# Twelve gate and up slices of layer 0's second half as seven block products, with the weight blocks added in SBUF by VectorE

## The chip, the cores and the metric

The kernel runs on one core of one Trainium2 chip. The metric is the device time of one execution in microseconds (us). Inside the core TensorE (PE) multiplies matrices into the eight PSUM banks, VectorE (DVE) and ScalarE (ACT) do elementwise work, GpSimd (POOL) and SyncE (SP) mainly issue DMA transfers here. Each engine works off its own instruction stream in order and waits on semaphores for the others.

## The reference: what is computed

One inference step of a two-layer decoder, for a prompt of 1024 tokens and 8 sample tokens, all in float32, with a model width of 1024. Each layer has a mixer (layer 0: a gated linear recurrence beside attention over 256 memory tokens; layer 1: stick-breaking attention beside memory attention) and then a SwiGLU feed-forward block, with RMSNorm around both:

```python
def swiglu(h, w_gu, w_down):
    gate, up = jnp.split(h @ w_gu, 2, axis=-1)
    return (jax.nn.silu(gate) * up) @ w_down

h = h + rmsnorm(mix, g[1])
h = h + rmsnorm(swiglu(rmsnorm(h, g[2]), w_gu[l], w_down[l]), g[3])
```

The feed-forward width is 2816, so `w_gu` has 2 x 2816 columns and `w_down` has 2816 rows. The change concerns `h @ w_gu` of layer 0 for half of the tokens.

## The kernel before

Tokens are worked on in two groups: group 0 holds prompt tokens 0 to 511, group 1 holds prompt tokens 512 to 1023 and the 8 sample tokens (520 columns, worked as two pieces of 260). Activations lie with the model width on the 128 partitions, in eight tiles of 128 rows.

Every float32 operand is kept as two halves in a reduced-precision matmul type: a high half (a copy that rounds) and a low half (what is left). A product of two such operands is three matmuls: high x high, high x low, low x high. Activations are split once by `split_to`. Weights are split as they are loaded, by `split_w`: a DMA on SP's queue brings 128 x 512 numbers (256 KB) into a tile `w` of the pool `wraw` (5 buffers), ACT copies the high half into a tile `ws` of the pool `wspl` (5 buffers; L260), and DVE subtracts to give the low half (L261).

The feed-forward block is cut into 22 slices of 128 columns, in five parts of 5, 5, 4, 4 and 4 slices (`PARTS`). For each slice of a part a plain slice does: gate product (`proj`, L274, 48 matmuls of 260 columns), SiLU from exp and ln (`silu`, L291 to L295), up product (another 48), product of the two (L703), split of the result into a tile `m` (L281, L282). After the slices of a part comes the down projection of the part: eight output blocks m, each with three matmuls per slice and piece, added into `r` by DVE (L447).

At the end of the kernel, layer 1's group 1 does slices 4 to 21 in another form (`ffn_w`, `gate_up_w`). Gate and up weights of a slice are seen as a 2 x 2 matrix of blocks (two halves of the model width, 512 rows each, by gate and up), and the activations as a 2 x 2 matrix (two halves of the width by two pieces of 260 tokens). The product takes seven block products instead of eight (Winograd's form of Strassen's scheme). Each block product j (0 to 6) is 12 matmuls of 260 columns (L552). Sums of activation blocks are made once by `sums_w`. Sums of weight blocks have been put into DRAM far ahead, by accumulating DMAs on POOL's queue (`weight_sums`): they run beside layer 0's group 1 feed-forward block, one step per generator call, each started by a tiny ACT copy (`rr`, L602) and a tiny POOL copy (`mk`, L603). The four PSUM accumulators of a slice are single banks, and the bank order is arranged so that ACT and DVE move partial sums between them while other products run.

The order of instructions is not that of the source. Python generators are woven together (`weave`), and a scheduler then orders each engine's stream by priorities and by its own estimate of when operands will be ready. What it settles on is fixed when the program is built: an engine that waits for its next instruction does not take a later one.

The stretch that the change touches, in the profile of before: group 1 of layer 0 does parts 0 and 1 beside the attention of layer 1's group 0 (`b0.sb`, `b0.mem`); then parts 2, 3 and 4 (slices 10 to 21), with only `weight_sums` beside them. The memory attention `mem_attn` has, for each pair of query blocks, scores (L862), a row maximum on DVE (L867), exp on ACT (L873), a scale on DVE (L879), transposes on PE (L889) and values (L903). PSUM is split into two two-bank tiles `mm`, three single banks `s` and one bank `ns`.

Of the kernel before, what the change touches and what calls it, by code (L numbers as in the profile page):

```python
# [9 lines left out]
F32 = mybir.dt.float32  # L10
F32R = mybir.dt.float32r
# [7 lines left out]
P = 128  # L19
# [5 lines left out]
def tile_decoder(  # L25
# [61 lines left out]
    def Q(i):  # L87
        return single[0].tile([P, 512], F32, tag=f"q{i}", name=nm("q"))
# [6 lines left out]
    def A(dt=F32):  # L95
        return apool.tile([P, 2, WID], dt, tag="a", name=nm("a"))
# [226 lines left out]
            out.append(x)  # L323
            yield

    def sums_w(xs, ops):

        n, h = NG[1], PW[1]  # L330
        for k in range(4):
            x0, x1 = xs[k], xs[k + 4]
            y = YT()
            if k % 2 == 0:
                z, u = YT(), YT()
            o = (k % 2) * h

            def full(x, c):
                t = B()
                nc.vector.tensor_add(t[:, :h], x[:, 0, c : c + h].bitcast(F32), x[:, 1, c : c + h].bitcast(F32))  # L340
# [13 lines left out]
            yield  # L354

    def YT():
        return xpool.tile([P, 2, NG[1]], F32R, tag="x0", name=nm("y"))

    def wo_tiles(g):
# [91 lines left out]
    class out_proj:  # L451


        def __init__(self, g, l, store, last=False):
            self.g, self.l, self.store, self.x, self.last = g, l, store, [], last
# [65 lines left out]
        split_to((mt[:, 0, :n], mt[:, 1, :n]), sg[:, :n])  # L521
        return mt, last

    def gate_up_w(l, f, ops, spl, raws):

        h, n = PW[1], NG[1]
        part, o = part_of(f)
        gate, up = f * P, DFF + f * P
        src = [
            (w_gu[l][0:512, gate : gate + P], 0), (sums[l][part][0][:, o : o + P], 4), (sums[l][part][1][:, o : o + P], 5),  # L530
            (w_gu[l][512:D, gate : gate + P], 1), (sums[l][part][2][:, o : o + P], 6), (sums[l][part][3][:, o : o + P], 2),
            (w_gu[l][512:D, up : up + P], 3),
        ]

        def weight(j):
            r = raws()
            nc.sync.dma_start(r, src[j][0].rearrange("(k p) m -> p k m", p=P))
            return r.rearrange("p k m -> p (k m)")

        def split(src):  # L540
            w = spl()
            nc.scalar.copy(w[:, 0, :], src)  # L542
            nc.vector.tensor_sub(w[:, 1, :], src, w[:, 0, :].bitcast(F32))  # L543
            return w

        def product(ps, j, first=False):
            w = split(weight(j))
            i = src[j][1]
            for k in range(4):
                x = ops[k][i]  # L550
                for wi, (wj, xi) in enumerate(((0, 0), (0, 1), (1, 0))):
                    nc.tensor.matmul(  # L552
                        ps[:, :h], w[:, wj, k * P : (k + 1) * P], x[:, xi, :],
                        start=(first and k == 0 and wi == 0), stop=(k == 3 and wi == 2), skip_group_check=True,
                    )

        pa, pb, pc, pd = (Q(i) for i in range(4))
        product(pa, 0, True)
        nc.scalar.activation(pb[:, :h], pa[:, :h], AF.Copy, scale=-1.0)
        product(pd, 1, True)  # L560
        product(pb, 2)
        nc.scalar.activation(pc[:, :h], pb[:, :h], AF.Copy, scale=-1.0)
        product(pa, 3)
        sg = T()
        nc.scalar.activation(sg[:, :h], pa[:, :h], AF.Silu)
        product(pb, 4)
        dt = T()
        nc.scalar.copy(dt[:, h:n], pd[:, :h])
        gt = T()
        nc.vector.tensor_add(gt[:, h:n], dt[:, h:n], pb[:, :h])  # L570
        product(pc, 5)
        nc.vector.tensor_sub(gt[:, :h], pc[:, :h], dt[:, h:n])
        product(pb, 6)
        nc.scalar.activation(sg[:, h:n], gt[:, :h], AF.Silu)
        nc.vector.tensor_mul(sg[:, :h], sg[:, :h], pb[:, :h])
        nc.vector.tensor_mul(sg[:, h:n], sg[:, h:n], gt[:, h:n])
        mt = M(F32R)
        split_to((mt[:, 0, :n], mt[:, 1, :n]), sg[:, :n])
        return mt

    sums = {}

# [32 lines left out]
    class ffn_w:  # L615


        def __init__(self, l, x, plain):
            self.g, self.l, self.x, self.ops, self.plain, self.n, self.r, self.pi = 1, l, x, [], plain, 0, 0, 0
            self.R = self.acc = None  # L620
            self.half = []
            self.sums = sums_w(x, self.ops)

        def spl(self):
            self.n += 1
# [13 lines left out]
        def part(self, pi):  # L639
            l, n, h = self.l, NG[1], PW[1]  # L640
            f0, nf = PARTS[pi]
            last = pi == len(PARTS) - 1
            mids = []
            for j in range(nf):
                self.pi = pi
                if f0 + j < self.plain:
                    mt, ins = gate_up_q(l, f0 + j, self.x)
                    mids.append(mt)
                    with tc.issue_after(ins.ins):
                        for _ in range((1, 2, 1, 0)[j]):  # L650
                            next(self.sums, None)
                else:
                    mids.append(gate_up_w(l, f0 + j, self.ops, self.spl, self.raws))
                yield
            if pi == 0:
                self.R = R_one()
            if last:
                self.acc = small([P, WID], tag="st", bufs=3)
                nc.scalar.preload_act_table_set("natural_log_exp_and_others")
            for m in range(ND):  # L660
                w = split_w(w_down[l], f0, nf, m * P)
                pp = [Q(2 * (m % 2) + a) for a in range(2)]
                for k in range(nf):
                    wh, wl = w[k]
                    for wi, (wt, xi) in enumerate(((wh, 0), (wh, 1), (wl, 0))):
                        for a in range(2):
                            nc.tensor.matmul(  # L667
                                pp[a][:, :h], wt, mids[k][:, xi, a * h : (a + 1) * h],
                                start=(k == 0 and wi == 0), stop=(k == nf - 1 and wi == 2),
                            )  # L670
                for a in range(2):
                    d = self.R[m][:, a * h : (a + 1) * h]
                    if pi == 0:
                        nc.scalar.copy(d, pp[a][:, :h])
                    else:
                        nc.vector.tensor_add(d, d, pp[a][:, :h])
                if last:
# [8 lines left out]
            yield from finish_rows(self)  # L686

    class ffn:
        def __init__(self, g, l, xt, rows=False):
            self.g, self.l, self.xt, self.rows = g, l, xt, rows  # L690
            self.R = self.acc = None

        def part(self, pi):
            g, l = self.g, self.l
# [2 lines left out]
            last = pi == len(PARTS) - 1  # L697
            mids = []
            for j in range(nf):
                pg = proj(g, w_gu[l], 0, ND, (f0 + j) * P, self.xt)  # L700
                sg = silu(None, pg, g)
                pu = proj(g, w_gu[l], 0, ND, DFF + (f0 + j) * P, self.xt)
                nc.vector.tensor_mul(sv(sg, g), sv(sg, g), pv(pu, g))  # L703
                mt = M(F32R)
                split_to((mt[:, 0, :n], mt[:, 1, :n]), sg[:, :n])
                mids.append(mt)
                self.now = sg[:, 0:1]
                yield
            if pi == 0:
                self.R = R_one()  # L710
            if last:
                self.acc = small([P, WID], tag="st", bufs=3)
            for m in range(ND):
# [3 lines left out]
                if last and self.rows:  # L717
# [3 lines left out]
                    if m == 3:  # L721
                        first_half(self)
                if m % 2:
                    yield

        def finish(self, store):
# [770 lines left out]
    b0 = mixer_b(0, xb0)  # L1497
    weave((b0.heads(), 8), (o1.finish(), 17))
    b0.open()
    f1 = ffn(1, 0, o1.x)  # L1500
    ws = weight_sums(1, range(5), lambda: f1.now)
    weave((chain(b0.sb(), b0.mem()), 24), (chain(f1.part(0), f1.part(1)), 18), (islice(ws, 16), 17))
    weave((chain(f1.part(2), f1.part(3), f1.part(4)), 24), (ws, 24))
# [55 lines left out]
```

## Time and profile before

| | |
|---|---|
| median of 3 runs | 2498.44 us (2496.12 to 2499.25) |
| the profiled execution's own time | 2499.1 us |
| its span | 2497.4 us |
| PE busy | 2462.8 us (99%), 15565 matmuls |
| DVE busy | 1571.8 us (63%) |
| ACT busy | 1183.0 us (47%) |
| DMA | 358.21 MB, 143 GB/s mean |

The span is from the first to the last instruction of one profiled execution; its own time has 1.7 us around that. Busy time is a union of the instructions' durations. A matmul's duration is its latency; since matmuls overlap, the pace is read from start to start. Views used below: busy time by stretches of time, groups of instructions by line, the chain of work that ended last, instructions in order of time, and DMA issues with their time to landing.

### The profile page before, as it was taken

What the parts mean: (1) busy time and instruction counts of PE and PEld (TensorE: products, weight loads), DVE (VectorE), ACT (ScalarE), POOL (GpSimd) and SP (SyncE); (2) the same over time, 40 slices, a digit from 0 to 9 for tenths busy, and PEclk for the clock granted to TensorE, in tenths of its full rate; (3) what the DMA queues carried; (4) which work ended last, traced back from release to release, by engine and by line L of the source; (5) the groups of instructions that cost most, each with busy time, mean ns of one, the idle gap of its engine ahead of it and who ended that gap; (6) DMA issues with size and microseconds to landing.
All of it is one profiled execution on the core that took longest, in us unless ns stands there. A gap on an engine that the chain in (4) does not pass through costs nothing.

```text
span 2497.4 us, 40764 instructions
## 1 busy us (share of the span) xinstructions
PE 2462.8 (99%) x15565; PEld 2169.9 (87%) x15565; DVE 1571.8 (63%) x2756; ACT 1183.0 (47%) x2277; POOL 98.3 (4%) x139
## 2 busy tenths in 40 slices
PE   8999999999999999999999999999999999999998
PEld 6888988877877897999999989877787797999997
DVE  5766556655765585655544575777577648755655
ACT  5446543243433454555433454555444445564444
POOL 1000000000000000010111100022000000000000
PEclk9999999999999999999999999999999999999999
DMA  5352252233643447586678976544454234365542
GB/s 186 114 165 68 72 156 81 60 110 116 184 124 98 129 138 227 156 195 177 173 191 215 234 193 196 160 142 138 121 149 130 85 115 122 121 192 145 151 137 69
DMA packets 496110, 358.21 MB, mean 143 GB/s; under 512 B 19110, under 2 KB 443635, under 8 KB 495915
## 3 DMA queue, kind: packets, MB, share of 16 engines
q1 hardware_dynamic: 477354, 301.08, 40.5%
q0 software_dynamic: 18560, 54.53, 9.1%
q8 instruction: 122, 2.00, 0.3%
q14 instruction: 74, 0.60, 0.1%
HBM read 325.73 MB, written 75.94 MB: 161 GB/s over the span
## 4 chain that ended last, share of the span: by engine, by line
PE 88%; DVE 5%; DMA 3%; ACT 2%; issue 2%; POOL 0%; SPq 0%; DVEq 0%; ACTq 0%; POOLq 0%
PE mm L274 59%; PE q L552 7%; PE q L667 5%; PE s L1180 2%; PE q L510 2%; PE mm L1048 2%; PE s L903 1%; PE s L862 1%; PE mm L812 1%; DMA b<-qd 1%; PE mm L839 1%; DVE ws L261 1%; PE ns L957 1%; PE s L1336 1%; DMA c<-in_cache_sb_v,pidx 1%
## 5 line engine op out<-in xcount | busy, mean ns | idle before, releaser
L274 PE MATMUL mm<-x,ws 128*128 128x260 f32 (+1 forms) x7776 | 1332.9, 330 | 0.0
L274 PEld LDWEIGHTS mm<-x,ws 128*128 128x128 f32 x7776 | 1148.3, 188 | 151.5 <-issue 12.0
L260 ACT CAST ws<-w 128x512 fp32r<-128x512 f32 x712 | 420.2, 591 | 763.2 <-PE mm L274 620.2
L261 DVE TENSOR_TENSOR ws<-w,ws 128x512 fp32r<-128x512 f32 x712 | 462.5, 653 | 286.8 <-ACT ws L260 278.3
L274 PE MATMUL mm<-m,ws 128*128 128x512 f32 (+1 forms) x2112 | 393.5, 343 | 0.1
L274 PEld LDWEIGHTS mm<-m,ws 128*128 128x128 f32 x2112 | 324.4, 189 | 49.9 <-issue 2.6
L667 PE MATMUL q<-m,ws 128*128 128x260 f32 x1056 | 128.8, 283 | 0.0
L667 PEld LDWEIGHTS q<-m,ws 128*128 128x128 f32 x1056 | 127.2, 188 | 0.4 <-ACT hT L485 0.2
L543 DVE TENSOR_TENSOR ws<-w,ws 128x512 fp32r<-128x512 f32 x126 | 86.6, 691 | 61.5 <-ACT ws L542 59.3
L552 PE MATMUL q<-y,ws 128*128 128x260 f32 x864 | 112.9, 283 | 0.0
L542 ACT CAST ws<-w 128x512 fp32r<-128x512 f32 x126 | 78.0, 621 | 69.6 <-PE q L667 27.4
L552 PEld LDWEIGHTS q<-y,ws 128*128 128x128 f32 x864 | 107.6, 189 | 0.0
L291 DVE TENSOR_SCALAR t<-mm 128x512 f32<-128x512 f32 (+1 forms) x82 | 56.7, 692 | 79.6 <-PE mm L274 79.6
L447 DVE TENSOR_TENSOR r<-r,mm 128x512 f32<-128x512 f32 (+1 forms) x96 | 66.0, 688 | 61.1 <-PE mm L274 60.3
L703 DVE TENSOR_TENSOR t<-t,mm 128x512 f32<-128x512 f32 (+1 forms) x66 | 45.5, 690 | 74.2 <-PE mm L274 73.9
L295 DVE TENSOR_TENSOR t<-t,t 128x512 f32<-128x512 f32 (+1 forms) x66 | 45.8, 694 | 70.6 <-ACT t L294 70.6
L552 PE MATMUL q<-x,ws 128*128 128x260 f32 x648 | 86.3, 282 | 0.0
L552 PEld LDWEIGHTS q<-x,ws 128*128 128x128 f32 x648 | 81.3, 188 | 0.0
L314 DVE TENSOR_TENSOR st<-st,n 128x512 f32<-128x512 f32 (+1 forms) x98 | 67.1, 691 | 8.8 <-ACT n L313 7.0
L281 ACT CAST m<-t 128x512 fp32r<-128x512 f32 (+1 forms) x88 | 54.9, 624 | 18.1 <-DVE t L703 8.9
L282 DVE TENSOR_TENSOR m<-t,m 128x512 fp32r<-128x512 f32 (+1 forms) x88 | 61.0, 693 | 2.6 <-ACT m L281 1.4
L984 POOL DMA_INDIRECT c<-in_cache_sb_k,pidx x16 | 16.4, 1026 | 1170.5 <-ACT n L313 958.6
(339 smaller groups left out, 2557.9 us busy)
## 6 DMA issues: line engine op xcount, KB each, us to landing
w<-in_w_gu SPq DMA_DIRECT2D x334, 256.0 KB, 3.4
w<-in_w_down SPq DMA_DIRECT2D x160, 256.0 KB, 3.5
w<-in_w_in_a SPq DMA_DIRECT2D x80, 256.0 KB, 3.0
wsum<-in_w_gu POOLq DMA_DIRECT2D x18, 1024.0 KB, 9.5
w<-wsum SPq DMA_DIRECT2D x72, 256.0 KB, 3.8
w<-in_w_o SPq DMA_DIRECT2D x64, 256.0 KB, 2.8
wsum<-in_w_gu POOLq DMA_DIRECT2D x12, 1280.0 KB, 10.7
w<-in_w_mem_kv SPq DMA_DIRECT2D x32, 256.0 KB, 3.2
```

What stands on the lines that cost most here:

```text
L260: nc.scalar.copy(ws[:, 0, :n, :], raw[:, :n, :])
L261: nc.vector.tensor_sub(ws[:, 1, :n, :], raw[:, :n, :], ws[:, 0, :n, :].bitcast(F32))
L274: nc.tensor.matmul(ps[:, a, : PW[g]], wt, xt[k][:, xi, o : o + PW[g]], start=(k == 0 and wi == 0), stop=(k == nk - 1 and wi == 2),)
L281: nc.scalar.copy(dst[0], src)
L282: nc.vector.tensor_sub(dst[1], src, dst[0].bitcast(F32))
L291: nc.vector.tensor_scalar(sv(x, g), pv(ps, g), -44.0, None, op0=ALU.max)
L314: nc.vector.tensor_add(acc[:, :n], acc[:, :n], t[:, :n])
L447: nc.vector.tensor_add(dst, dst, pv(ps, g))
L542: nc.scalar.copy(w[:, 0, :], src)
L543: nc.vector.tensor_sub(w[:, 1, :], src, w[:, 0, :].bitcast(F32))
L552: nc.tensor.matmul(ps[:, :h], w[:, wj, k * P : (k + 1) * P], x[:, xi, :], start=(first and k == 0 and wi == 0), stop=(k == 3 and wi == 2), ...
L667: nc.tensor.matmul(pp[a][:, :h], wt, mids[k][:, xi, a * h : (a + 1) * h], start=(k == 0 and wi == 0), stop=(k == nf - 1 and wi == 2),)
```

## The change

The class `ffn` of layer 0 gets a number `prod`, the first slice to be done as block products; group 1 of layer 0 is made with `prod=10`, so parts 2, 3 and 4 use them. `gate_up_w` is made general: it is given a function that yields the weight block for product j, and a function that yields the four accumulators. For layer 0 these are:

- `sums_here`: the four weight blocks a11, a12 (gate), a21, a22 (up) of a slice are loaded in four DMAs of 256 KB into two tiles `c` of the pool `cpool` (4 buffers, shared with attention), one with a11 and a12, one with a21 and a22. DVE makes the sums: a21+a22, a11+a21, the latter plus a22, and that plus a12, in four tiles `b` of the pool `bpool`.
- accumulators: two single banks `s` and the two halves of a two-bank tile `mm`.
- `sums_w` is run for the activations of layer 0's group 1 too, during the down projection of part 1, into tiles `a` of the pool `apool`.
- The SiLU of these slices is ACT's own function, as in layer 1, so ACT's function table is loaded once before and once after.

Everything after layer 0 is unchanged but for the names of arguments. The loads of the paged cache for layer 1 (`cache_sb_k`, POOL's queue), which use `cpool` too, come out later in POOL's stream: before, eight of them stood ahead of and among the sums of weights; now these eight stand among the last sums.

```diff
-    def gate_up_w(l, f, ops, spl, raws):
...
+    def sums_here(l, f, raws, outs):
+        a11, a12, a21, a22 = raws()
+        for r, k0, m0 in (
+            (a11, 0, f * P), (a21, 0, DFF + f * P), (a12, 512, f * P), (a22, 512, DFF + f * P),
+        ):
+            nc.sync.dma_start(
+                r.rearrange("p (k m) -> p k m", m=P), w_gu[l][k0 : k0 + 512, m0 : m0 + P].rearrange("(k p) m -> p k m", p=P)
+            )
+        kept = {}
+
+        def add(a, b):
+            t = outs()
+            nc.vector.tensor_add(t, a, b)
+            return t
+
+        def weight(j):
+            if j == 1:
+                return add(a21, a22)
+            if j == 2:
+                kept[3] = add(a11, a21)
+                kept[2] = add(kept[3], a22)
+                return kept[2]
+            if j == 4:
+                return kept[3]
+            if j == 5:
+                return add(kept[2], a12)
+            return (a11, None, None, a12, None, None, a22)[j]
+
+        return weight
+
+    def gate_up_w(weight, ops, spl, quads):
...
-        pa, pb, pc, pd = (Q(i) for i in range(4))
+        pa, pb, pc, pd = quads()
...
     class ffn:
-        def __init__(self, g, l, xt, rows=False):
-            self.g, self.l, self.xt, self.rows = g, l, xt, rows
+        def __init__(self, g, l, xt, rows=False, prod=NF):
+            self.g, self.l, self.xt, self.rows, self.prod = g, l, xt, rows, prod
             self.R = self.acc = None
+            self.ops = []
+            self.sums = sums_w(xt, self.ops, lambda: A(F32R))
+
+        def raws(self):
+            ts = [C(), C()]
+            return [t[:, a, :] for t in ts for a in range(2)]
+
+        def quads(self):
+            t = mmp.tile([P, 2, 512], F32, tag="mm", name=nm("mm"))
+            return S(), t[:, 0, :], t[:, 1, :], S()
...
+                if f0 + j >= self.prod:
+                    mt, gate = gate_up_w(
+                        sums_here(l, f0 + j, self.raws, B),
+                        self.ops, lambda: wspl.tile([P, 2, 512], F32R, tag="ws", name=nm("ws")), self.quads,
+                    )
+                    mids.append(mt)
+                    self.now = mt[:, 0, 0:1].bitcast(F32)
+                    yield
+                    continue
...
+            if last and self.prod < NF:
+                with tc.issue_after(gate.ins):
+                    nc.scalar.preload_act_table_set("natural_log_exp_and_others")
...
                 if m % 2:
+                    if f0 + nf == self.prod < NF:
+                        next(self.sums, None)
                     yield
...
-    f1 = ffn(1, 0, o1.x)
+    f1 = ffn(1, 0, o1.x, prod=10)
```

More of the change, by code (lines that the diff above doesn't have):

```diff
@@ L324, in normed, with sums_w @@
             yield
-    def sums_w(xs, ops):
+    def sums_w(xs, ops, YT):
         n, h = NG[1], PW[1]
@@ L354, in sums_w, with Y0 @@
             yield
-    def YT():
+    def Y0():
         return xpool.tile([P, 2, NG[1]], F32R, tag="x0", name=nm("y"))
@@ L522, in gate_up_q, with sums_stored @@
         return mt, last
-    def gate_up_w(l, f, ops, spl, raws):
-        h, n = PW[1], NG[1]
+    def sums_stored(l, f, raws):
         part, o = part_of(f)
         gate, up = f * P, DFF + f * P
+        s1, s2, s3, s4 = (t[:, o : o + P] for t in sums[l][part])
         src = [
-            (w_gu[l][0:512, gate : gate + P], 0), (sums[l][part][0][:, o : o + P], 4), (sums[l][part][1][:, o : o + P], 5),
-            (w_gu[l][512:D, gate : gate + P], 1), (sums[l][part][2][:, o : o + P], 6), (sums[l][part][3][:, o : o + P], 2),
-            (w_gu[l][512:D, up : up + P], 3),
+            w_gu[l][0:512, gate : gate + P], s1, s2, w_gu[l][512:D, gate : gate + P], s3, s4,
+            w_gu[l][512:D, up : up + P],
         ]
@@ L536, in weight @@
             r = raws()
-            nc.sync.dma_start(r, src[j][0].rearrange("(k p) m -> p k m", p=P))
+            nc.sync.dma_start(r, src[j].rearrange("(k p) m -> p k m", p=P))
             return r.rearrange("p k m -> p (k m)")
+        return weight
[24 more added lines that the diff above has]
+            return (a11, None, None, a12, None, None, a22)[j]
+        return weight
+    def gate_up_w(weight, ops, spl, quads):
+        h, n = PW[1], NG[1]
+        src = (0, 4, 5, 1, 6, 2, 3)
         def split(src):
@@ L547, in product @@
             w = split(weight(j))
-            i = src[j][1]
+            i = src[j]
             for k in range(4):
@@ L573, in gate_up_w @@
         product(pb, 6)
-        nc.scalar.activation(sg[:, h:n], gt[:, :h], AF.Silu)
+        last = nc.scalar.activation(sg[:, h:n], gt[:, :h], AF.Silu)
         nc.vector.tensor_mul(sg[:, :h], sg[:, :h], pb[:, :h])
@@ L578, in gate_up_w @@
         split_to((mt[:, 0, :n], mt[:, 1, :n]), sg[:, :n])
-        return mt
+        return mt, last
     sums = {}
@@ L621, in __init__ @@
             self.half = []
-            self.sums = sums_w(x, self.ops)
+            self.sums = sums_w(x, self.ops, Y0)
         def spl(self):
@@ L652, in part @@
                 else:
-                    mids.append(gate_up_w(l, f0 + j, self.ops, self.spl, self.raws))
+                    mids.append(gate_up_w(
+                        sums_stored(l, f0 + j, self.raws), self.ops, self.spl, lambda: [Q(i) for i in range(4)]
+                    )[0])
                 yield
```

## The prediction

> **What bounds the kernel now.** I read the page's totals first, then the chain that ended last over the stretch that the change touches, then busy time by stretches.
>
> ```profile
> span 2497.4 us, 40764 instructions
> PE 2462.8 (99%) x15565; PEld 2169.9 (87%) x15565; DVE 1571.8 (63%) x2756; ACT 1183.0 (47%) x2277; POOL 98.3 (4%) x139
> ```
>
> ```profile
> 1241.31 209.76 PE mm L274 x1730
> ```
>
> ```profile
> 1196.00:1241.00 45.00, 44.93 (x336) 42.60 (x334) 24.47 (x52) 19.17 (x51) 5.50 (x8) 1.00 0.76 182
> 1241.00:1450.00 209.00, 209.00 (x1729) 208.11 (x1728) 104.84 (x153) 84.49 (x154) 31.05 (x47) 1.00 0.84 213
> 2480.00:2497.00 17.00, 6.43 (x42) 4.69 (x40) 8.69 (x14) 5.20 (x9) 0.00 (x0) 0.65 0.32 125
> ```
>
> The columns of the last view are stretch, length, busy time and count of PE, PEld, DVE, ACT and POOL, granted clock, DMA share, GB/s. From 1241 to 1451 us (parts 2 to 4 of layer 0's group 1, slices 10 to 21) the chain is 1730 matmuls and nothing else: TensorE never waits, and VectorE is half busy. Matmuls taken out here shorten the kernel one for one, as long as nothing new makes TensorE wait. The question is what does.
>
> **The change, part by part.**
>
> *Matmuls removed.* A slice drops from 96 matmuls to 84. Both forms stand in this trace: two plain slices by their L703, two product slices by their first products.
>
> ```profile
> 1250.19 0.70 DVE L703 TENSOR_TENSOR t<-t,mm 128x520 f32<-128x520 f32 x1 [1.51 <-PE mm L274]
> 1261.67 0.70 DVE L703 TENSOR_TENSOR t<-t,mm 128x520 f32<-128x520 f32 x1 [1.52 <-PE mm L274]
> ```
>
> ```profile
> 2299.79 3.06 PE L552 MATMUL q<-y,ws 128*128 128x260 f32 x24
> 2304.12 1.61 PE L552 MATMUL q<-y,ws 128*128 128x260 f32 x12
> 2305.57 1.60 PE L552 MATMUL q<-x,ws 128*128 128x260 f32 x12
> ...
> 2309.88 3.06 PE L552 MATMUL q<-y,ws 128*128 128x260 f32 x24
> ```
>
> 11.48 us against 10.09 us: 1.39 us a slice, for twelve slices **-16.7 us**. A product takes 1.45 us, a matmul 10.09 / 84 = 0.120 us.
>
> *Work added on VectorE and ScalarE.* Spacing of operations that follow each other at once:
>
> ```profile
> 1234.30 0.69 DVE L447 TENSOR_TENSOR r<-r,mm 128x520 f32<-128x520 f32 x1
> 1234.91 0.69 DVE L261 TENSOR_TENSOR ws<-w,ws 128x512 fp32r<-128x512 f32 x1
> 1235.51 0.68 DVE L282 TENSOR_TENSOR x<-s,x 128x512 fp32r<-128x512 f32 x1
> 1236.11 0.68 DVE L867 TENSOR_REDUCE nmx<-s 128x2 f32<-128x512 f32 x1
> ```
>
> ```profile
> 2308.46 0.42 DVE L576 TENSOR_TENSOR t<-t,t 128x260 f32<-128x260 f32 x1
> 2308.80 0.42 DVE L575 TENSOR_TENSOR t<-t,q 128x260 f32<-128x260 f32 x1
> ```
>
> ```profile
> L260 ACT CAST ws<-w 128x512 fp32r<-128x512 f32 x648 | 401.2, 620 | 665.2 <-PE mm L274 550.0 <-issue 34.0 <-PE mm L1048 12.3
> L517 ACT ACT_TABLE_LOAD x1 | 1.3, 1283 | 0.0
> ```
>
> So 0.6 us for 512 columns, 0.34 us for 260. A product slice has 12 of the first (seven splits, four adds, the split of `m`) and four of the second: 8.6 us of VectorE in 10.09 us. By throughput it fits, with 1.5 us to spare. ScalarE has eight casts and five short copies, about 7 us, and two table loads of 1.3 us; these hide behind the waits below, and would cost up to 2.6 us without them.
>
> *The weight loads.* This is the part that decides. `cpool` holds two slices. The tile with a21 and a22 of slice n is free only after VectorE's last split of that slice (a22, product 6); only then can SP load slice n+2 into it. On VectorE, in the built program, the add a21+a22 of slice n+2 stands five instructions behind that split, and ahead of everything that slice n+1 still needs:
>
> ```
> split a22 of slice 14          <- frees the tile, load of slice 16 starts
> splits 0, 1, 2 of slice 15, one 260-column add
> a21+a22 of slice 16            <- waits for that load
> a11+a21 of 16, a 260-column subtraction, +a22 of 16, split 3 of slice 15,
> a 260-column product, split 4, a 260-column product, split 5, +a12 of 16,
> split of m (slice 14), split a22 of slice 15
> ```
>
> The queue is in order, so each slice costs VectorE at least W, the wait from the one split to the landed pair of loads, plus what runs from that add to the next such split: nine operations of 0.6 us and three of 0.34 us, 6.5 us. W has no row of its own; the rows nearest are single loads of the same 256 KB in the same stretch, beside the sums of weights, and in the last stretch, without them.
>
> ```profile
> w<-in_w_gu SPq DMA_DIRECT2D x35, 256.0 KB, 6.7
> wsum<-in_w_gu POOLq DMA_DIRECT2D x16, 1024.0 KB, 9.3
> ```
>
> ```profile
> w<-in_w_gu SPq DMA_DIRECT2D x28, 256.0 KB, 3.4
> ```
>
> ```profile
> DMA to landing us min/median/max: 3.4/5.8/8.2
> ```
>
> ```profile
> GB/s 130 284 124 181 241 88 155 247 127 186 337 227 158 245 222 237 163 310 253 263 164 119 170 246 107 207 377 168 208 239 273 113 211 368 203 284 136 83 205 354
> ```
>
> Before, these loads run five buffers (some 14 us) ahead, and 6.7 us hurts nobody. Now W stands in a loop. I take 6.7 us for the first load and 0.7 us for the second behind it (256 KB at the 377 GB/s of the busiest slice): **W = 7.4 us**, because each tile is freed just as the slice's `m` starts the next sum of weights. Bounds: 4.1 us (3.4 + 0.7, no sum beside it) and 8.9 us (8.2 + 0.7). A turn is then 7.4 + 6.5 = 13.9 us, against the 10.09 us that TensorE needs and the 11.48 us of before.
>
> Worked through part 3 (slices 14 to 17), from its first product. Slices 14 and 15 were loaded during the down projection. Five `ws` buffers let split 6 of slice 14 follow the end of the second product: 2.9 + cast 0.62 + split 0.6 = 4.2 us. Then split 6 of slices 15, 16, 17 at 18.1, 32.0 and 45.9 us. The next add waits W again, for slice 19, and ahead of slice 17's last subtraction and products: four operations of 0.6 us, three of 0.34 us and a cast, 4.1 us, until slice 17's `m` is there at 45.9 + 7.4 + 4.1 = 57.4 us. TensorE, unhindered, asks for it after four slices and 24 matmuls of the down projection, 360 x 0.120 = 43.2 us. Loss: 14.2 us, about six of them in one piece at that end.
>
> Part 2 has one wait more: slice 11's tile is held by the memory attention until 2.3 us after its last scaling. From there 2.3 + W + 2.4 + W + 3.7 + W + 6.5 + W + 6.5 + W + 4.1 = 62.5 us (short runs first, since the queue is still filling), against 44.4 us: 18.1 us. Part 4 has nothing to load behind slice 21, so two waits: 4.2 + W + 6.5 + W + 4.1, and 1.8 us on ScalarE until product 4 of slice 20 has its accumulator, 31.4 us, against 216 x 0.120 = 25.9 us: 5.5 us. Sum: 18.1 + 14.2 + 5.5 = **+37.8 us**, which is 11 W - 43.6.
>
> *Sums of activations, end of the memory attention.* 48 operations of 260 columns, 16 us of VectorE, enter the stretch from 1196 to 1241 us, where 24.5 of 45 us are busy. They fit, but the attention's short chain queues behind them, and the plain matmuls that filled its gaps are gone:
>
> ```profile
> 1234.81 1.03 PE L862 MATMUL s<-c,a 128*128 128x256 f32 x4
> 1236.48 2.14 PE L274 MATMUL mm<-x,ws 128*128 128x260 f32 x15
> 1238.69 0.33 PE L889 MATMUL s<-ident,b 128*128 128x128 f32 x1
> ```
>
> Last scores (done at 1235.84) to transposes are 2.85 us; now only 0.5 us of values can stand in them: 2.3 us. The pair before gets about 1.2 us later by the operations put ahead of its maximum. **+3.5 us**; bounds 0 (all in VectorE's slack) and 16 (all on the path); I stay near the low end, since the slack of 20 us is larger than the work.
>
> *Moved.* SP issues as many loads as before; the last three of each down projection now stand behind the tile freed by the part's last split (45.9 us above), and are needed after 57 us: nothing. The cache loads on POOL move to about 1430 us and wait there for `c` tiles, with `mk` copies and sums of weights behind them; the next such load of before runs at 1615 us, and the sums are read after 2200 us: nothing.
>
> ```profile
> 1615.46 1.26 POOL L984 DMA_INDIRECT c<-in_cache_sb_k,pidx  x1 [157.49 <-DVE sc L944]
> ```
>
> Sum: -16.7 + 37.8 + 3.5 = +24.6 us on the profiled execution's 2499.1 us, which is 0.7 us above the median of the runs: **2524 us**.
>
> **The rivals.**
>
> *The loads land in time (faster).* If W stays under 5.2 us (11 x 5.2 - 43.6 - 16.7 + 3.5 = 0), the sign turns. For it: 3.4 us, the fastest load here and the median of the last stretch; slices get longer, so sums of weights lie less densely. Against: each load starts together with a sum, whose own 9.3 us cover it. At W = 4.1 us only part 2 loses, 1.5 us: 2499.1 - 16.7 + 1.5 + 3.5 = 2487 us.
>
> *In between.* W near 5.2 us: 2499 us.
>
> *Pairs queue.* Two pairs per slice are in flight together, and the sum is in the way of all of them. At W = 8.9 us: 2524 + 11 x 1.5 = 2540 us.
>
> *The clock falls in the waits.* In the last row of stretches above, with TensorE mostly idle, the granted clock is 0.65. If the two waits of some 6 us at part ends and the one of 4 us in slice 10 bring it there for as long again, matmuls in those 16 us take 1 / 0.65: +8.6 us, 2533 us. Against: no row of this trace shows it for waits that short. The Trainium skill (TensorE: Matmul & The Clock Gate, section "HAM oscillation — how this bites in real kernels") says that idle gaps above some 3.4 us, here those three, bring half clock; by its 3.4 us at half rate after each, an estimate, the sum would be 3 x 1.7 = 5 us more. No run shown yet can tell.
>
> *The change does not save its matmuls:* excluded by the 10.09 us that the same form takes in layer 1.
>
> **How the numbers follow.** Forecast 0.48 (W 6 to 8.2, 2509 to 2533 us); pairs queue 0.20; the clock 0.09; in between 0.08; in time 0.15, most of it clearly faster. A measurement of this kernel tells about 0.2% (5 us) from no change. Faster 0.14, same 0.08, slower 0.78. Range 2497 to 2541 us: from the middle case to the upper bound of W; it leaves out most of the faster case and the far ends.
>
> **What would show it.** Right: matmuls down by 144; the adds of a21+a22 wait for DMA, 2 to 5 us each, with TensorE's idle time in those parts ended by VectorE; product slices about 13.9 us apart; idle pieces of some 6 us before the down projections of parts 2 and 3; a span of the parts near 1241 to 1470 us. Wrong: products 1.45 us apart throughout, or those loads landing under 5 us; a lower granted clock between 1241 and 1480 us would speak for the fourth rival.

## The result, and the profile after

The changed kernel takes 2527.4 us (median of six runs, 2521.3 to 2532.4), the kernel before 2498.4 us (2496.1 to 2499.3): 1.0117 times as long, interval 1.0102 to 1.0133, so 29 us slower. The prediction was 2524 us. The profiled execution took 2524.87 us, its span is 2523.0 us, 25.6 us more than before. Totals of the page, then the stretches, with the columns of before:

```profile
span 2523.0 us, 40632 instructions
PE 2459.1 (97%) x15421; PEld 2162.1 (86%) x15421; DVE 1628.9 (65%) x2900; ACT 1206.7 (48%) x2355; POOL 98.3 (4%) x139
```

```profile
1196.00:1241.00 45.00, 43.49 (x321) 40.84 (x320) 38.32 (x95) 24.48 (x65) 2.18 (x4) 1.00 0.66 157
1241.00:1480.00 239.00, 209.18 (x1584) 202.96 (x1584) 145.28 (x247) 102.03 (x217) 37.73 (x54) 0.94 0.75 193
```

144 matmuls are gone, yet TensorE is busy only 3.7 us less: between 1241 and 1480 us it stands idle for 29.8 us, where in the kernel before it never stood until the parts were done, and its granted clock there is 0.94. The waits of that stretch (who waited for what: total, times, longest), and a piece of the chain that ended last in part 3:

```profile
DVE b L552 <- DMA c<-in_w_gu: 31.0, 10, 6.4
PE mm L587 <- DVE t L607: 28.3, 9, 6.3
```

```profile
1324.37 0.70 DVE ws L578
1325.50 4.63 DMA c<-in_w_gu
1330.22 1.29 DVE b L552 x2
...
1336.22 0.61 DVE ws L578
1337.26 6.32 DMA c<-in_w_gu
1343.68 1.29 DVE b L552 x2
...
1350.93 0.61 DVE ws L578
1351.97 6.27 DMA c<-in_w_gu
1358.33 1.29 DVE b L552 x2
...
1364.32 0.61 DVE ws L578
1365.36 9.43 DMA c<-in_w_gu
1374.89 1.29 DVE b L552 x2
```

This is the loop: last split of a slice (L578), load, add (L552), work to the next such split. From add to add it turns in 13.5, 14.7 and 16.6 us. From the end of the split to the add, the W of the prediction, are 5.2, 6.9, 6.8 and 10.0 us, 7.2 on average. TensorE's own rows, with the idle time before each in brackets:

```profile
1262.56 2.43 PE L587 MATMUL mm<-a,ws 128*128 128x260 f32 x12 [2.33 <-DVE t L607]
1276.85 2.95 PE L587 MATMUL mm<-a,ws 128*128 128x260 f32 x12 [2.21 <-DVE t L607]
1295.18 2.97 PE L587 MATMUL mm<-a,ws 128*128 128x260 f32 x12 [6.25 <-DVE t L607]
...
1345.36 2.97 PE L587 MATMUL mm<-a,ws 128*128 128x260 f32 x12 [2.91 <-DVE t L607]
1360.01 1.72 PE L587 MATMUL mm<-a,ws 128*128 128x260 f32 x12 [2.69 <-DVE t L607]
1376.58 2.97 PE L587 MATMUL mm<-a,ws 128*128 128x260 f32 x12 [6.01 <-DVE t L607]
...
1428.67 1.70 PE L587 MATMUL mm<-a,ws 128*128 128x260 f32 x12 [3.45 <-DVE t L607]
```

Every long wait stands before product 6, two of 6 us at the ends of parts 2 and 3. And in five of these seven rows the twelve matmuls behind the wait take 2.4 to 3.0 us, not the 1.7 us of the other two: these waits cost time twice, once as idle time and once in the matmuls behind them. What differs is the granted clock (third number from the end) in the stretches behind the waits, here two that cost twice and the one of 3.45 us that does not:

```profile
1295.10:1298.00 2.90, 2.82 (x13) 2.82 (x14) 1.56 (x4) 0.42 (x1) 0.00 (x0) 0.50 0.04 12
1376.50:1379.40 2.90, 2.83 (x13) 2.83 (x14) 1.56 (x4) 0.42 (x1) 0.00 (x0) 0.50 0.07 16
1428.60:1431.40 2.80, 2.73 (x22) 2.73 (x23) 2.80 (x7) 1.82 (x4) 1.29 (x1) 1.00 0.00 0
```

The stretch ends with the first matmul of the final norm (L303), which starts when part 4 is done; it is called the parts' end below. Before, then changed:

```profile
1450.90 1.02 PE L303 MATMUL ns<-st,ones 128*128 128x512 f32 x2
```

```profile
1478.97 1.02 PE L303 MATMUL ns<-st,ones 128*128 128x512 f32 x2
```

The parts end 28.1 us later; the rest of the kernel is 2.5 us shorter, and why stays open.

### The profile page after: what moved, and what is told of

Read it like the earlier page. It is cut to its first block, busy times and chain, and to the rows that moved or that the text cites. A ratio compares the mean times of both kernels' runs of the same rounds, so it can differ in the third digit from the quotient of the medians.

```text
span 2523.0 us, 40632 instructions
## 1 busy us (share of the span) xinstructions
PE 2459.1 (97%) x15421; PEld 2162.1 (86%) x15421; DVE 1628.9 (65%) x2900; ACT 1206.7 (48%) x2355; POOL 98.3 (4%) x139
## 4 chain that ended last, share of the span: by engine, by line
PE 86%; DVE 6%; DMA 4%; ACT 2%; issue 1%; SPq 0%; POOL 0%; DVEq 0%; ACTq 0%
PE mm L274 55%; PE q L587 7%; PE q L704 5%; DMA c<-in_w_gu 3%; PE s L1241 2%; PE q L510 2%; PE mm L1109 2%; PE s L964 1%; PE s L923 1%; DMA b<-qd 1%; PE mm L587 1%; PE mm L873 1%; PE ns L1018 1%; PE mm L900 1%; PE s L1397 1%
## 5 line engine op out<-in xcount | busy, mean ns | idle before, releaser
L274 PE MATMUL mm<-x,ws 128*128 128x512 f32 (+1 forms) x6624 | 1193.5, 338 | 0.0
L274 PEld LDWEIGHTS mm<-x,ws 128*128 128x128 f32 x6624 | 1009.4, 188 | 152.0 <-issue 12.0
L260 ACT CAST ws<-w 128x512 fp32r<-128x512 f32 (+1 forms) x664 | 390.3, 589 | 659.5 <-PE mm L274 511.1
L261 DVE TENSOR_TENSOR ws<-w,ws 128x512 fp32r<-128x512 f32 (+1 forms) x664 | 429.0, 649 | 269.6 <-ACT ws L260 264.8
L578 DVE TENSOR_TENSOR ws<-w,ws 128x512 fp32r<-128x512 f32 x126 | 86.5, 691 | 61.9 <-ACT ws L577 57.6
L577 ACT CAST ws<-w 128x512 fp32r<-128x512 f32 x126 | 77.9, 621 | 71.1 <-PE q L704 26.0
L587 PE MATMUL mm<-a,ws 128*128 128x260 f32 x432 | 64.8, 304 | 28.3 <-DVE t L607 28.3
L291 DVE TENSOR_SCALAR t<-mm 128x512 f32<-128x512 f32 (+1 forms) x70 | 48.3, 690 | 61.9 <-PE mm L274 61.7
L587 PEld LDWEIGHTS mm<-a,ws 128*128 128x128 f32 x432 | 59.6, 206 | 30.6 <-DVE t L607 30.1
L759 DVE TENSOR_TENSOR t<-t,mm 128x512 f32<-128x512 f32 (+1 forms) x54 | 37.2, 688 | 55.5 <-PE mm L274 55.0
L638 POOL COPY mk<-rr 128x1 f32<-128x1 f32 x40 | 14.7, 368 | 1343.8 <-ACT rr L637 1331.1
```

The source lines that it names most:

```text
L260: nc.scalar.copy(ws[:, 0, :n, :], raw[:, :n, :])
L261: nc.vector.tensor_sub(ws[:, 1, :n, :], raw[:, :n, :], ws[:, 0, :n, :].bitcast(F32))
L274: nc.tensor.matmul(ps[:, a, : PW[g]], wt, xt[k][:, xi, o : o + PW[g]], start=(k == 0 and wi == 0), stop=(k == nk - 1 and wi == 2),)
L587: nc.tensor.matmul(ps[:, :h], w[:, wj, k * P : (k + 1) * P], x[:, xi, :], start=(first and k == 0 and wi == 0), stop=(k == 3 and wi == 2), ...
```

## The experiments

All times are medians, the parts' ends are those of one profiled execution each; the kernel before took 2498.3 us beside e1 to e7, 2496.4 beside e8 and e9, 2498.5 beside e10 and e11.

| kernel | time, us | parts' end, us |
|---|---|---|
| before | 2498.4 | 1450.9 |
| changed | 2527.4 | 1479.0 |
| e1 add later | 2487.8 | 1441.8 |
| e2 deeper loads | 2494.9 | 1447.5 |
| e3 sums of weights later | 2510.6 | 1443.4 |
| e4 part 4 only | 2495.9 | 1449.9 |
| e5 sums of activations alone | 2497.8 | 1450.5 |
| e6 matmuls in the waits | 2533.2 | 1487.1 |
| e7 three delays (one run) | 2516.3 | 1472.0 |
| e8 three delays, filled | 2511.9 | 1468.0 |
| e9 add later, deeper loads | 2487.6 | 1439.6 |
| e10 other banks | 2519.7 | 1473.0 |
| e11 add later, other banks | 2491.1 | 1444.6 |

**e1: the place of the add.** In `sums_here`, with `last_split` set by `split`:

```diff
             if j == 1:
-                return add(a21, a22)
+                with tc.issue_after(last_split[0].ins) if last_split else ExitStack():
+                    return add(a21, a22)
```

> Everything is computed; only VectorE's order changes: the add a21+a22 of a slice is queued behind the last split of the slice before, so the wait for a landing no longer stands ahead of work that the slice before still needs. The loads, their buffers and the sums of weights stay as they are. Queue theory (the loss is the place of the add in an in-order queue): the load has some 10 us from one slice's last split to the next slice's, against landings of 5 to 10 us in the changed kernel, so the waits of DVE on c<-in_w_gu fall from 6.4 us to under 2 us, TensorE's 29.8 us of idle time between 1241 and 1480 us to under 6 us, and the time to 2498.4 - 16.7 (matmuls) + 3.5 (sums of activations) + 1.5 (slice 11's held tile) = 2487 us, range 2482 to 2496. Rival, the loads themselves are the limit (landings get as late as the queue allows): slices stay 13 us or more apart, 2515 to 2527 us. Rival, VectorE's 8.6 us of work in 10.09 us does not fit in practice: slices 10.6 to 11 us apart, 2493 to 2498 us, with idle time of TensorE ended by VectorE and no DMA behind it.

Measured: 2487.8 us, 0.9960 of before (0.9947 to 0.9972), faster than both kernels. In VectorE's waits no DMA is left, and TensorE is busy throughout (the three largest of VectorE's waits from 1241 to 1442 us; then the stretch):

```profile
DVE ws L261 <- ACT ws L260: 16.7, 17, 3.2
DVE r L447 <- PE mm L274: 14.5, 14, 1.5
DVE ws L581 <- ACT ws L580: 11.5, 21, 1.0
```

```profile
1241.00:1442.00 201.00, 199.98 (x1605) 195.87 (x1604) 148.38 (x251) 103.73 (x221) 37.40 (x53) 1.00 0.88 230
```

Loads, buffers, sums of weights and VectorE's operations are those of the changed kernel. Their order differs: with the add that the edit names, the other three adds of the slice stand behind the last split of the slice before, too. This place in the queue is worth 37.2 us at the parts' end. VectorE's 8.6 us of work in a turn of 10 us does fit: 148.4 of 201 us busy.

**e2: loads earlier, the add in its place.**

```diff
-            ts = [C(), C()]
-            return [t[:, a, :] for t in ts for a in range(2)]
+            t = C()
+            ws = [wraw.tile([P, 4, P], F32, tag="w", name=nm("w")) for _ in range(2)]
+            return [t[:, 0, :], t[:, 1, :]] + [w.rearrange("p k m -> p (k m)") for w in ws]
```

> Everything is computed; only the buffers of the raw weights change: a11 and a12 of a slice still share one tile of cpool, a21 and a22 take two of the five wraw buffers, so cpool holds four slices and wraw two and a half, and a21+a22 of slice n+2 no longer waits for the last split of slice n. Queue theory: the loop of split, load and add is cut at the load's start, so the same gain as with the add put later: 2487 us, range 2482 to 2496, no wait of DVE on c or w above 2 us. If the late add gives that gain and this one does not, loads started earlier do not help (they queue among themselves), and the place of the add is what counts. Rival, the loads are the limit: 2515 to 2527 us. One new wait is possible: loads of w_down now share wraw with a21 and a22; if they come late, idle time before the down projections ended by ws<-w, up to 3 us in each of three parts.

Measured: 2494.9 us, 0.9991 (0.9982 to 1.0001). 31.4 of the 37.2 us come back, so cutting the loop at its other end works too. The new wait I named is there, though at another instruction: the next part's add, not a load of `w_down`, waits in the down projections of parts 2 and 3 (two of four such waits). TensorE stands idle in them for 5.0 us in four pieces, most of the 5.8 us by which the parts end later than in e1.

```profile
1290.71 0.69 DVE L552 TENSOR_TENSOR b<-w,w 128x512 f32<-128x512 f32 x1 [1.93 <-DMA w<-in_w_gu]
...
1358.73 0.69 DVE L552 TENSOR_TENSOR b<-w,w 128x512 f32<-128x512 f32 x1 [2.02 <-DMA w<-in_w_gu]
```

**e3: the sums of weights out of the stretch.** The last 24 of 40 are woven into layer 1's group 0:

```diff
-    weave((chain(f1.part(2), f1.part(3), f1.part(4)), 24), (ws, 24))
+    drain(f1.part(2), f1.part(3), f1.part(4))
...
-        (chain(f0.part(0), f0.part(1), f0.part(2), f0.part(3)), 34),
+        (chain(f0.part(0), f0.part(1), f0.part(2), f0.part(3)), 34), (ws, 24),
```

> Everything is computed; the last 24 of the 40 sums of weights (1 MB each, on POOL's queue) are issued in layer 1's group 0 instead of beside the product slices. VectorE's order and the buffers stay. Sums theory (W is long because a 1 MB sum runs beside each pair): W falls from 5 to 10 us to 4.1 us (3.4 + 0.7), so the parts' span shrinks by nearly all of its idle time, TensorE idle between 1241 and the parts' end 2 to 6 us instead of 29.8, and the parts end near 1447 us instead of 1479 us. Pairs theory (the pair and the next loads share the queue whatever runs beside): W stays at 6 us or more, the parts end at 1465 us or later. The whole time also has what the moved sums do to layer 1, where POOL's queue holds the loads of the cache: 2487 us if nothing, more if those loads get late; the verdict on W is therefore read from the parts' end, not from the total.

Measured: the parts end at 1443.4 us, and VectorE's waits for these loads between 1241 and 1480 us shrink from 31.0 us to

```profile
DVE b L552 <- DMA c<-in_w_gu: 3.2, 6, 1.4
```

In the chain the loads' pieces are now 3.5 to 4.7 us. So W is long because a sum of weights runs beside the pairs; with W near 4.5 us the same loop costs next to nothing. The total, 2510.6 us (1.0044, 1.0028 to 1.0061), is worse than before by what happens in layer 1, where the sums now lie beside the loads of the cache: from the parts' end on the profiled execution takes 1069 us instead of 1046. Ten of these 23 us are idle time of TensorE in one stretch, 3.6 us before (first row) and now 14.0 us; which transfer holds which there was not tried.

```profile
1700.00:1900.00 200.00, 196.37 (x899) 150.57 (x898) 143.69 (x218) 94.92 (x180) 10.28 (x8) 0.99 0.44 129
```

```profile
1700.00:1900.00 200.00, 185.96 (x830) 141.98 (x829) 130.20 (x196) 87.83 (x176) 22.17 (x29) 0.96 0.66 179
```

**e4: part 4 alone** (`prod=18`).

> Everything is computed; products only from slice 18 on (part 4), the sums of activations under part 3's down projection. My sum for part 4 alone: 48 matmuls fewer (-5.6), two waits of W (+5.5), and the sums of activations, 16 us of VectorE beside 23 us of matmuls with some 10 us of its own work there (+0 to +3): 2498 to 2501 us, the same as before within 0.2%. Rival, every product slice costs alike (29 us over 12 slices): +9.7, 2508 us. Rival, the loss comes with the end of the memory attention or slice 11's held tile: 2493 us, since neither touches part 4.

Measured: 2495.9 us, 0.9991 (0.9982 to 1.0001): no loss, 2 us under my forecast; that every product slice costs alike (2508 us) is out. The third case (2493 us) is as near as my forecast, and e4 does not tell the two apart: VectorE waits for a load there only once, for 3.7 us, where the sum has two waits of W.

**e5: the sums of activations alone** (`if False:` in place of `if f0 + j >= self.prod:`, and no table load behind part 4).

> Everything is computed; all slices keep the plain form of before, but the 48 operations that sum the activations for the products stay where the change puts them, in part 1's down projection beside the end of the memory attention; their results are unused. It prices the second term of my sum by itself. As I worked it out (the attention's short chain queues behind them): +3.5 us, 2502 us. Rival, they cost only because the plain matmuls that filled the attention's gaps are gone, and here these are back: 2498 us, TensorE idle under 0.3 us between 1196 and 1241 us. The upper bound, all of it on the path: +16, 2514 us.

Measured: 2497.8 us, 0.9999 (0.9989 to 1.0008). By themselves they cost nothing: TensorE is busy 44.93 of the 45 us from 1196 to 1241 us, as before. In the changed kernel 1.5 us are idle there, so that wait needs the second condition too: the plain matmuls that filled the attention's gaps are gone. What their loss costs without the sums no run shows.

**e6: work put into the waits of the changed kernel.** Behind product 6 of slices 10 to 20 (`fill` is 2 there, and 0 in slice 21):

```diff
-        product(pb, 6)
+        w6 = product(pb, 6)
+        for _ in range(fill):
+            for k in range(4):
+                for wi, (wj, xi) in enumerate(((0, 0), (0, 1), (1, 0))):
+                    nc.tensor.matmul(
+                        pd[:, :h], w6[:, wj, k * P : (k + 1) * P], ops[k][3][:, xi, :],
...
```

> The changed kernel with more work: behind product 6 of each product slice but the last, 24 matmuls (2.9 us at full rate) with product 6's weights into the accumulator pd, which is free by then; their result is unused. Loads and VectorE's work are the same, so the loop of split, load and add is the same, and TensorE's idle time per turn falls from some 4 us to some 1 us. Clock theory (7 to 8 of the 37 us lost come from matmuls at a lower clock after waits of more than 3 us; the waits alone are 30 us): with the waits filled, the granted clock between 1241 and 1480 us rises from 0.94 to 0.98 or more, and the time falls although 264 matmuls were added: 2520 to 2523 us. Waits theory (all 37 us are time of the loop, and the low clock lies in time that is lost anyway): 2527 us. Rival, the added 32 us of matmuls stand on the path (TensorE, not VectorE, comes last in many turns): 2533 us or more.

Measured: 2533.2 us, the third case. The clock between 1241 and 1480 us rose from 0.94 to 0.98, but the matmuls stood on the path, and some of VectorE's operations changed places. It decides nothing on the clock; e7 and e8 do.

**e7 and e8: the price of a wait.** e7 is e1 with delays on VectorE ahead of split 3 of slices 12, 16 and 20; e8 puts matmuls into those waits:

```diff
+    IDLE = {12: 9, 16: 13, 20: 22}
...
+            if j == 3 and f in IDLE:
+                t = outs()
+                nc.vector.tensor_copy(t, a12)
+                for _ in range(IDLE[f]):
+                    nc.vector.tensor_max(t, t, t)
+                return t
```

> Everything is computed: the kernel with the add put later, which has no waits in this stretch, with three delays put in on VectorE: ahead of split 3 in slices 12, 16 and 20 a chain of 10, 14 and 23 operations of 512 columns (some 6, 8 and 14 us at 0.6 us). VectorE runs 2 to 4 us ahead there, so TensorE stands idle about 2 to 3, 5 and 10 us. It prices a wait by itself. Clock theory: behind the two long waits the next product takes near 3 us instead of 1.45 to 1.65, some 2 to 3 us more per wait in all; behind the short one it does not. Rival: matmuls go at full rate at once after each, the granted clock is low only within the idle time.

> The kernel with three delays on VectorE again, with 24, 48 and 108 matmuls (2.9, 5.8 and 13.0 us) put on TensorE into those three waits, behind product 2 of slices 12, 16 and 20, from weights that are there, into a free bank; their result is unused. The delays themselves and VectorE's order are nearly the same, and the added matmuls are shorter than the waits (4.1, 7.0 and 13.8 us), so nothing but the clock is to change. Clock theory (the three waits, 24.7 us, moved the parts' end by 30.2 us, from 1441.8 to 1472.0; the other 5.5 us are products at half rate behind the waits): with 180 matmuls more the parts end near 1466.5 us, the next products take 1.45 to 1.7 us, and the time falls by 5.5 us, from 2516.3 to 2511 us. Rival (the 5.5 us are VectorE's time to catch up, not the clock): the parts end at 1472 us or later, the time stays at 2516 us.

Measured in e7: waits of 4.1, 7.0 and 13.6 us, 24.7 in all, move the parts' end by 30.3 us against e1. The shortest was to be 2 to 3 us, so e7 prices no wait as short as those of the changed kernel that cost twice. TensorE's first wait, and the same place in e8, with e8's third wait below the dots:

```profile
1269.55 0.80 PE L599 MATMUL s<-x,ws 128*128 128x260 f32 x2 [4.11 <-ACT ws L588]
1270.15 0.51 PE L599 MATMUL mm<-a,ws 128*128 128x260 f32 x1
1270.45 2.37 PE L599 MATMUL s<-x,ws 128*128 128x260 f32 x10
1272.62 2.58 PE L599 MATMUL mm<-a,ws 128*128 128x260 f32 x11
1275.00 1.19 PE L599 MATMUL s<-x,ws 128*128 128x260 f32 x8
```

```profile
1264.80 3.07 PE L615 MATMUL ns<-a,ws 128*128 128x260 f32 x24
1269.05 0.51 PE L599 MATMUL s<-x,ws 128*128 128x260 f32 x2 [1.18 <-ACT ws L588]
...
1406.15 13.13 PE L615 MATMUL ns<-a,ws 128*128 128x260 f32 x108
1419.86 0.51 PE L599 MATMUL s<-x,ws 128*128 128x260 f32 x2 [0.58 <-ACT ws L588]
```

In e7 24 matmuls take 5.5 us, 1269.55 to 1275.0, with a granted clock of 0.50; at 0.12 us each they need 2.9. With 180 matmuls more, e8 reaches the product behind the third wait at 1419.86 us instead of 1425.26, and takes 2511.9 us instead of 2516.3 (e7 has one run only, and the kernel before took 1.8 us less beside e8 than beside e7, so the parts' ends are the better measure). The clock theory holds, at some 2.5 us for each of the first two waits. At the parts' end 4.0 of the 5.6 us are left, since part 4's down projection then waits for a cast of its weights, 1.9 us in one piece.

**e9: both cures together.**

> Everything is computed; the add put later and the deeper loads of raw weights together. Theory (with the add later no wait for a landing is left in the parts, so earlier loads have nothing to give, and a21 and a22 in wraw wait behind w_down's buffers at each part's start): 2488 to 2494 us, not faster than the add later alone (2487.8 us); waits of DVE on w<-in_w_gu of 4 to 6 us per part start if they cost. Rival (landings still set the pace somewhere): 2480 to 2485 us.

Measured: 2487.6 us, 0.9963 (0.9949 to 0.9977): the same as e1 within the intervals. Once the add is out of the way, earlier loads have nothing to give.

**e10 and e11: the accumulators' places exchanged**, in the changed kernel and in e1.

```diff
-            return S(), t[:, 0, :], t[:, 1, :], S()
+            return t[:, 0, :], S(), S(), t[:, 1, :]
```

> The changed kernel, everything computed, with the accumulators' places exchanged: pb and pc, which products 2 and 4 to 6 write and VectorE's last operations read, take the two small banks, pa and pd share the two-bank tile. In the changed kernel nearly all of TensorE's idle time ends with the subtraction t<-mm,t (L607), which reads pc, while product 6 writes pb in the same tile. VectorE keeps all its operations and the wait of the add; some 260-column operations and additions change places around it. Queue theory (what TensorE waits for in the end is the add in VectorE's queue; the subtraction only stands behind it): the idle time then ends at other instructions (a split, or m), the loop stays as long, 2520 to 2528 us. Bank theory (product 6 is held by a reader of the other half of its tile, and this is a good share of the 28.8 us): idle time before product 6 goes away and the time falls to 2510 us or less.

> The add put later and the accumulators exchanged, everything computed. Queue theory: with the add later no idle time before product 6 is left (0.1 us between 1241 and 1400 us), so the banks have nothing to give: 2486 to 2490 us. Bank theory: product 6 is still held a little in each slice (product slices 10.07 to 10.3 us apart, 10.09 in the last stretch): up to 2 us less, 2485 us.

Against what I wrote, these two compute other values than the reference: pb and pc begin as values that ScalarE writes, and it may be that in these banks not all of those are added to. Instructions are the same, so they tell of time only. The Trainium skill (PSUM — Partial Sum Buffer, section "PSUM: the matmul accumulator") says that a matmul which does not start a group adds only where an earlier matmul set a status bit, and that ScalarE's writes do not set it. The small banks last held 256 columns of the attention, pb has 260; that this is the reason no run here shows.

Measured: e10 2519.7 us, e11 2491.1 us. In e10 the long waits leave product 6, which both theories say, but they turn up elsewhere, as the queue theory has it: before `m` and at ScalarE's first value of pb:

```profile
1263.74 2.97 PE L587 MATMUL mm<-a,ws 128*128 128x260 f32 x12 [2.58 <-ACT s L594]
...
1292.84 23.22 PE L274 MATMUL mm<-m,ws 128*128 128x260 f32 x174 [5.39 <-ACT m L281]
```

The 7.7 us that e10 gains are not pinned to the banks: VectorE's order changed with them, and its waits for the loads are 21.1 us instead of 31.0. e11 is slower than e1 by 3.3 us, outside both forecasts, with half a microsecond before ScalarE's value in nearly every slice. So the two-bank tile decides where TensorE is seen to wait, not that it waits.

## Why the prediction was right, step by step

*The loop of split, load and add: right, in place and in size.* W was to be 7.4 us; in part 3 it is 7.2 on average. The run from add to next split was to be 6.5 us; it is 6.6 (1330.22 to 1336.83), 7.9 and 6.6. Turns were to be 13.9 us; they are 13.5, 14.7 and 16.6. e1 and e2 cut the loop at its two ends, and e3 shortens W; each brings back 31 to 37 us at the parts' end.

*Its cost, +37.8 us: the sum is right, one of its parts is not.* Between the changed kernel and e1 the parts' end moves by 37.2 us. But 28.8 of them are idle time (29.8 against 1.0 from 1241 to 1480 us), and the other 8.4, by difference, are matmuls at a lower clock. The rows agree: with the matmuls that follow, the five costly waits lose 1.5, 1.5, 2.1, 1.4 and 2.3 us against the same places without a wait, about 9 us in all. In part 2 I had 18.1 us, and 11.9 are idle; part 3 14.2 and 12.3; part 4 5.5 and 5.7. The step that failed is part 2's "one wait more": slice 11's add starts without any wait,

```profile
1242.54 0.69 DVE L552 TENSOR_TENSOR b<-c 128x512 f32<-128x512 f32 x1
1243.15 0.69 DVE L552 TENSOR_TENSOR b<-c,c 128x512 f32<-128x512 f32 x1
```

its last loads were issued about when I said, at 1238.6 us, but had landed by 1242.5, behind VectorE's other work, and I had charged a full W for them. (The 44.4 us that I subtracted in part 2 I had not worked out; 360 matmuls are 43.2.) That took out about one W, and the clock, which the sum does not have, put back as much. That 37.8 meets 37.2 is luck.

*The rival of the clock: real, and wrongly left out of the sum.* I gave it 0.09, because no row of before showed it for waits that short. It is there: 8.6 us was its price by the row of the last stretch, 8.4 us is what the difference gives. That the two meet is luck as well: I had three waits and 16 us at a clock of 0.65, and there are five, with shorter stretches at 0.50. The five pay for it, three of them 2.2 to 2.9 us long, while ones of 2.69 and 3.45 us do not. The Trainium skill (TensorE: Matmul & The Clock Gate, section "HAM oscillation — how this bites in real kernels") has gaps above some 3.4 us as the condition, by which three waits would pay 5 us, an estimate; with that the rows differ. The Trainium skill says on the same page (TensorE: Matmul & The Clock Gate, section "What's actually happening") that the window in which activity is watched runs freely. If the limit depends on where in the window a gap falls, that would fit the rows, but no run here tests it.

*The end of parts 2 and 3.* About six microseconds in one piece: 6.25 and 6.01. They stand before product 6 of the last slice rather than before `m`, since product 6 waits for the subtraction L607 behind the add.

*Matmuls removed, -16.7 us: too much by 4.* From the first matmul of part 3 to the first of part 4 the kernel before takes 69.0 us (first fence), e1, where nothing hinders the products, 64.7 us (second): 4.2 us less a part, 12.7 us for the three.

```profile
1307.47 46.07 PE L274 MATMUL mm<-x,ws 128*128 128x260 f32 x384
...
1376.42 46.08 PE L274 MATMUL mm<-x,ws 128*128 128x260 f32 x384
```

```profile
1305.76 1.61 PE L591 MATMUL s<-x,ws 128*128 128x260 f32 x12
...
1370.49 1.60 PE L591 MATMUL s<-x,ws 128*128 128x260 f32 x12
```

Slices follow each other in 10.3 us there, not in the 10.09 us of layer 1; the rest, some 0.5 us a part, lies where slices and down projection meet.

*Sums of activations, end of the attention, +3.5 us: right in kind.* 1.5 us idle to 1241 us and 0.5 us behind it are what the rows show; e5 says that the sums alone cost nothing. *Moved loads: nothing*, as forecast; e3 shows that sums of weights do cost time when they are moved into layer 1.

*The whole.* By the rows the parts' 28.1 us are -12.7 for matmuls, 37.2 for the loop and its clock and 1.5 at the end of the attention, and 2.1 are left, of which 0.9 is a wait in e1's last down projection. With the 2.5 us that the rest of the kernel is shorter, the forecast of 24.6 us met the profiled 25.6 by errors of both signs.

*Rivals.* Loads in time (W under 5.2 us) is what e3 makes, and then the kernel's parts are indeed faster than before, 1443.4 against 1450.9 us. Pairs that queue are out: with the sums gone (e3), pairs land in 3.5 to 4.7 us.

## What to carry to other kernels

Before an operation that waits for a load is put into an in-order queue, look at what stands behind it: if the load's buffer is freed by something behind the operation of one turn earlier, wait and work add up in every turn, and moving the operation behind that work can bring it back (here all 37 us, and a slower kernel became the faster one). Price a load in a loop by its landing beside whatever large transfers run there, not by its landing alone. And a wait of TensorE of more than two microseconds can cost some 1.3 to 2.6 us more in the matmuls behind it, as five of seven did here and the three of e7.

## What the runs showed of the hardware that I had not expected

What the lower clock costs does not grow with the wait: behind 4.1 us in e7 24 matmuls run at half rate (granted clock 0.50), behind 13.6 us only the first 13 do (pieces of e7's chain).

```profile
1425.26 0.80 PE s L599 x2
1426.37 2.17 PE s L599 x10
1428.54 1.46 PE mm L599 x11
```

And filling a wait with matmuls whose result nobody reads can make a kernel faster: e8 does 180 more than e7, and its parts end 4.0 us earlier.
